# FFN second half as Strassen products over pairs of token tiles, with ff stored by token tile

## The chip, the cores and the metric

The kernel runs on one core of one Trainium2 chip. The metric is the device time of one execution in microseconds. An execution of the kernel before takes 2890.57 us (median of 3 runs, 2889.32 to 2894.1). Names used below: TensorE multiplies matrices into PSUM banks, VectorE and ScalarE work element by element, GpSimd here adds weight blocks and issues some transfers, SyncE (SP) issues most transfers.

## The reference, cut to what matters

An encoder layer (gated recurrence beside dilated attention, both gated by a condition), then a SwiGLU FFN, then a final norm. Two requests of 1024 and 512 tokens are worked on as one matrix of 1536 tokens. Only the FFN and the last norm bear on the change:

```python
D_MODEL = 1024; D_FF = 2816          # 22 column tiles of 128
h2 = _rmsnorm(x, norm2_g) * (1 + sc2) + sh2
fg, fu = jnp.split(h2 @ w_ffn_in, 2, axis=-1)
ff = (silu(fg) * fu) @ w_ffn_out     # (1536, 2816) @ (2816, 1024)
x = x + gt2 * ff
y = _rmsnorm(x, final_g)             # x * rsqrt(mean(x*x) + EPS) * final_g
```

All arrays are float32.

## The kernel before, in words

Every float32 product is made of three TensorE matmuls: each operand is split into a high part (a ScalarE copy to the type fp32r) and a low part (a VectorE subtraction of the high part), and hi x hi, hi x lo and lo x hi are accumulated. `split` (L146 to L149) does this.

The order of all work is written out by hand: instructions stand on each engine in the order of the code, and the engine works them off in that order.

**FFN first half** (L1382 on). 44 steps `p`: 22 column tiles in a first pass over tokens 0 to 767, and again in a second pass over tokens 768 to 1535 (`p % NFF` is the column tile, `p // NFF` the pass). Each step has 7 products `c` of 12 matmuls, Strassen's scheme over halves of the contraction and of the tokens, 384 columns each. The bank of a product is `(P1, P2, P3, P4, P1, P2, P3)[c]`; the fifth to seventh products accumulate onto a bank whose earlier content VectorE or ScalarE has already read. The evacuations are the `if c == ...` chain (L1392 to L1412). At c == 6 the two results, X (tokens of the first half of the pass) and Y (second half), are done and are stored by SP to `ffd`, which is laid out [column tile, 128, token]. `build` makes the weight operands of the products nine products ahead: GpSimd adds two blocks, ScalarE copies, VectorE subtracts. `wraw` loads the weights of a later step into tiles of the tags raw, hi and lo.

**FFN second half** (L1448 on). Three chunks of 512 tokens. For each chunk 11 steps `kp` over pairs of contraction tiles; in each step the transposed ff of 512 tokens (class `Stream`, 512 KB) and two rows of tiles of `w_fo` (class `Slots`, 1 MB) are loaded by SP, split, and multiplied: 4 token tiles by 2 halves of 512 output columns by 2 contraction tiles by 3 matmuls. All 8 PSUM banks are accumulators for the whole chunk, and w_fo is loaded and split again for each chunk. After a chunk `scale` multiplies the banks with the gate gt2 into SBUF, and `post` (run one per step of the next chunk) adds the residual x1, squares with accumulation, makes the reciprocal root (`rstd`, small VectorE operations around one ScalarE root), scales by final_g and stores through GpSimd. The last chunk's last two steps go token tile by token tile, with `post_half` and `post_last` behind them.

Of the kernel before, what the change touches and what calls it, by code (L numbers as in the profile page):

```python
# [10 lines left out]
F32 = mybir.dt.float32  # L11
# [6 lines left out]
P = 128  # L18
# [33 lines left out]
def encoder_kernel(  # L52
# [18 lines left out]
    ffd = dram("ffd", [NFF, P, T])  # L71
# [1157 lines left out]
    ffs = Stream([ffd[2 * n:2 * n + 2, :, cc * CH:(cc + 1) * CH].rearrange("k p n -> p k n")  # L1229
                  for cc in range(NCH) for n in range(NFF // 2)], shape=(P, 2, CH))  # L1230

    class Slots:

        def __init__(self):
            self.nl = self.ns = 0
            self.n = NCH * NFF // 2
            self.raw = None

        def at(self, i):
            a = slot[(3, 2, 1)[i % 3]].rearrange("p (a k n) -> p a k n", a=2, k=2)  # L1240
            return a[:, 0], a[:, 1]

        def load(self, n):
            if self.nl == 0:
                self.first = [wts.tile([P, D], F32, tag="lo", name="foraw") for _ in range(2)]
                for k in range(2):
                    sp.dma_start(out=self.first[k], in_=w_fo[k])
                self.nl = 1
            if self.raw is None and n > 1:
                self.raw = act1.tile([P, 2, 2, D], F32, tag="a", name="foraw")  # L1250
            while self.nl < min(n, self.n):
                kp = 2 * (self.nl % (NFF // 2))
                sp.dma_start(out=self.raw[:, self.nl % 2], in_=w_fo[kp:kp + 2].rearrange("k p n -> p k n"))
                self.nl += 1

        def split(self, n):
            while self.ns < min(n, self.n):
                hi, lo = self.at(self.ns)
                for k in range(2):
                    split(self.raw[:, self.ns % 2, k] if self.ns else self.first[k], hi[:, k], lo[:, k])  # L1260
                self.ns += 1

        def get(self, i):
            self.load(i + 1)
            self.split(i + 1)
            return self.at(i)

        def ahead(self, i):
            self.load(i + 2)
            self.split(i + 2)  # L1270
            self.load(i + 3)
# [363 lines left out]
```

## Time and profile before

| | |
|---|---|
| median of 3 runs | 2890.57 us |
| profiled execution, its own time | 2890.56 us |
| its span | 2888.8 us |
| TensorE busy | 2831.2 us, 98% |
| VectorE busy | 1794.3 us, 62% |
| ScalarE busy | 1182.5 us, 41% |
| GpSimd busy | 551.4 us, 19% |
| TensorE's mean granted clock | 0.991 of full |
| moved by DMA | 316.88 MB, 110 GB/s over the span |

The span runs from the first to the last instruction that the profiler recorded. Busy time is the time in which an engine had at least one instruction under way; a matmul's end is modelled, so that the pace of matmuls is better read from how many there are in a stretch than from the length of one. "Idle before" is the engine's idle time ahead of an instruction, with the engine or transfer whose signal ended it. A transfer's time to landing runs from its issue to the signal that its data has arrived.

### The profile page before, as it was taken

How to read it: one execution, taken by the hardware profiler on the slowest of the kernel's cores; microseconds unless marked ns; L12 is line 12 of the kernel's file. 1: busy time of each engine (PE TensorE's matmuls, PEld its weight loads, DVE VectorE, ACT ScalarE, POOL GpSimd, SP SyncE). 2: the span in 40 equal slices, each digit the busy share in tenths (PEclk: the TensorE clock that was granted, in tenths of full speed). 3: DMA queues.
4: the chain of work that ended last, by engine and by line, in shares of the span. 5: the costliest groups of instructions: out<-in, count | busy, mean ns of one | idle time of the engine just before them, and what ended most of it. 6: DMA issues, size and time to landing. Idle time of an engine off the chain costs nothing. (4 is left out here: it accounts for less than half of the span.)

```text
span 2888.8 us, 37337 instructions
## 1 busy us (share of the span) xinstructions
PE 2831.2 (98%) x14330; PEld 2375.9 (82%) x14330; DVE 1794.3 (62%) x3097; ACT 1182.5 (41%) x2260; POOL 551.4 (19%) x545
## 2 busy tenths in 40 slices
PE   8999999999999999999999999999999999999998
PEld 4878777877777777777778777899999999988886
DVE  6487776555555555553467846677788788635364
ACT  6375666333333333234431015544444334323232
POOL 0000000000000000000243331266544444300001
PEclk9999999999999999999999999999999999999999
DMA  6211011201111111111467754546434333355552
GB/s 235 68 35 66 33 55 45 78 30 34 34 35 37 41 34 35 34 35 54 130 228 259 245 181 130 178 158 188 141 104 166 101 101 101 133 208 167 189 173 90
DMA packets 125155, 316.88 MB, mean 110 GB/s; under 512 B 17096, under 2 KB 48328, under 8 KB 124720
## 3 DMA queue, kind: packets, MB, share of 16 engines
q1 hardware_dynamic: 106736, 252.30, 26.9%
q0 software_dynamic: 17664, 61.14, 6.1%
q8 instruction: 113, 1.85, 0.3%
q10 hardware_dynamic: 576, 1.05, 0.1%
q14 instruction: 66, 0.54, 0.1%
HBM read 242.57 MB, written 71.88 MB: 109 GB/s over the span
## 5 line engine op out<-in xcount | busy, mean ns | idle before, releaser
L158 PE MATMUL mm<-hh,whi 128*128 128x512 f32 x1632 | 663.6, 407 | 1.8 <-DVE hh L291 1.3
L160 PE MATMUL mm<-hh,wlo 128*128 128x512 f32 x1632 | 641.9, 393 | 0.0
L159 PE MATMUL mm<-hl,whi 128*128 128x512 f32 x1632 | 640.7, 393 | 0.5 <-DVE hl L292 0.4
L149 DVE TENSOR_TENSOR wlo<-wraw,whi 128x1024 fp32r<-128x1024 f32 x127 | 155.6, 1230 | 363.9 <-ACT whi L148 363.6
L158 PEld LDWEIGHTS mm<-hh,whi 128*128 128x128 f32 x1632 | 311.8, 191 | 70.4 <-issue 7.2
L160 PEld LDWEIGHTS mm<-hh,wlo 128*128 128x128 f32 x1632 | 308.2, 189 | 68.6
L159 PEld LDWEIGHTS mm<-hl,whi 128*128 128x128 f32 x1632 | 309.4, 190 | 62.6 <-DVE hl L292 3.3
L1296 POOL TENSOR_TENSOR sum<-wf 128x512 f32<-128x512 f32 x220 | 297.7, 1359 | 304.6 <-DVE woh L1307 192.8
L148 ACT CAST whi<-wraw 128x1024 fp32r<-128x1024 f32 (+1 forms) x129 | 131.1, 1017 | 406.5 <-PE sd L1474 175.0
L746 ACT ACTIVATE sm<-sm,sg 128x192 f32<-128x192 f32 (+2 forms) x288 | 114.3, 398 | 303.4 <-DVE sg L741 302.8
L1307 DVE TENSOR_TENSOR woh<-sum,woh 128x512 fp32r<-128x512 f32 x148 | 146.6, 1001 | 48.5 <-ACT woh L1306 48.1
L741 DVE CUSTOM_DVE_ANT_0 sm<-sd,mk 128x192 f32<-128x192 f32 (+2 forms) x288 | 72.9, 291 | 117.0 <-PE sd L734 64.3
L667 DVE SCALAR_TENSOR_TENSOR t<-mm,rp 128x512 f32<-128x512 f32 x72 | 49.8, 692 | 150.3 <-PE mm L160 150.3
L798 POOL DMA_DIRECT2D od<-of x24 | 13.1, 547 | 635.3 <-ACT qb L719 354.4
L1306 ACT CAST woh<-sum 128x512 fp32r<-128x512 f32 x148 | 91.5, 621 | 103.7 <-POOL sum L1296 103.7
L1378 PE MATMUL mm<-top,woh 128*128 128x384 f32 x348 | 116.5, 335 | 3.2 <-ACT top L1367 3.2
L1380 PE MATMUL mm<-top,woh 128*128 128x384 f32 x348 | 116.3, 334 | 0.0
L1379 PE MATMUL mm<-top,woh 128*128 128x384 f32 x348 | 116.2, 334 | 0.0
L856 DVE CUSTOM_DVE_ANT_0 jk<-ada 128x1024 bf16<-128x1024 f32 x64 | 80.5, 1270 | 24.4 <-DMA ada<-in_w_ada_dram 17.2
L1474 PE MATMUL mm<-wol,whi 128*128 128x512 f32 x352 | 94.5, 390 | 0.1
L1474 PE MATMUL sd<-wol,whi 128*128 128x512 f32 x352 | 94.4, 389 | 0.0
L1405 ACT ACTIVATE flat<-flat 128x384 f32<-128x384 f32 x44 | 23.1, 526 | 169.4 <-DVE flat L1404 169.4
(341 smaller groups left out, 6230.2 us busy)
## 6 DMA issues: line engine op xcount, KB each, us to landing
wf<-in_w_fi_dram SPq DMA_DIRECT2D x88, 512.0 KB, 4.5
wraw<-in_w_in_dram SPq DMA_DIRECT2D x68, 512.0 KB, 3.5
foraw<-in_w_fo_dram SPq DMA_DIRECT2D x32, 1024.0 KB, 5.2
ffd<-flat SPq DMA_DIRECT2D x88, 192.0 KB, 4.3
wraw<-ffd SPq DMA_DIRECT2D x33, 512.0 KB, 3.6
ada<-in_w_ada_dram SPq DMA_DIRECT2D x32, 512.0 KB, 3.8
gated<-gs POOLq DMA_DIRECT2D x48, 256.0 KB, 2.7
gt<-gated POOLq DMA_DIRECT2D x48, 256.0 KB, 4.0
```

Of the source, the lines that this page charges most:

```text
L148: s.copy(out=hi, in_=t)
L149: eng.tensor_tensor(out=lo, in0=t, in1=hi.bitcast(F32), op=ALU.subtract)
L158: pe.matmul(ps, lhsT=hi(k), rhs=xh(k), start=a, stop=False)
L159: pe.matmul(ps, lhsT=hi(k), rhs=xl(k), start=False, stop=False)
L160: pe.matmul(ps, lhsT=lo(k), rhs=xh(k), start=False, stop=z)
L746: s.activation(out=sm[:, c], in_=sm[:, c], func=AF.Exp, scale=-1.0, bias=sg[:, u, x:x + 1], accum_out=sg[:, u, x + 1:x + 2])
L1296: g_.tensor_tensor(out=sums[m], in0=wraws[p, a], in1=wraws[p, b], op=op)
L1307: v.tensor_tensor(out=r[:, CH:], in0=t, in1=f32(r[:, :CH]), op=ALU.subtract)
L1378: pe.matmul(ps, lhsT=hi, rhs=bh[:, k], start=k == 0 and not more, stop=False, skip_group_check=more)
L1379: pe.matmul(ps, lhsT=hi, rhs=bl[:, k], start=False, stop=False, skip_group_check=more)
L1380: pe.matmul(ps, lhsT=lo, rhs=bh[:, k], start=False, stop=k == 3, skip_group_check=more)
L1474: pe.matmul(pp[t][e], lhsT=lt[:, k2, cols], rhs=w[:, k2, e * CH:(e + 1) * CH], start=(k == 0 and lt is fh and w is wh), stop=(k == NFF - 1 ...
```

## The change

The first half's arithmetic stays. Its steps take the column tiles in another order (`column`: 0, 11, 1, 12, ...), ff is stored by token tile, [token tile, 128, 22 x 128], and beside it `ffx` holds for each pair of token tiles (t, t + 3) two differences and a sum of blocks of ff. With A11, A12 the two column halves of ff of token tile t, A21, A22 those of token tile t + 3: d0 = A21 - A11, d1 = A12 - A22, s = A21 + A22. VectorE makes them at c == 6 (one operation at even steps, two at odd) and SP stores them.

The second half becomes 7 combinations by 6 pairs of token tiles, 42 steps; a step is one product of 11 contraction tiles by 3 matmuls of 512 columns into one PSUM bank, with its left operand `acmb` (two buffers) and its B pieces (`bslot`, 20 slots). `aload` loads raw left operands two steps ahead, `aprep` splits them one step ahead (in two combinations it adds two operands first, in three pieces); `bload` and `bbuild` load and make B pieces (for five of the seven combinations the sum or difference of two blocks of w_fo) one combination ahead, in a pair of raw buffers. `take` adds the product of the step before into accumulators in SBUF (one tile of 128 x 1024 for each of the 12 token tiles), and as soon as a half of a token tile is complete, `half` applies gate and residual and squares, and `fin` normalises a token tile and stores it. The last product is done in two halves of 256 columns with a short chain behind them.

Cut to its core; of the removed code only the heads are left:

```diff
-    ffd = dram("ffd", [NFF, P, T])
+    ffd = dram("ffd", [NT, P, NFF * P])
+    ffx = dram("ffx", [NT // 2, 3, P, NFF // 2 * P])
...
-    ffs = Stream([ffd[2 * n:2 * n + 2, :, cc * CH:(cc + 1) * CH].rearrange("k p n -> p k n")
-    class Slots:
-    fos = Slots()
...
+    PRODO = (
+        (3, ("11",), ("12", "22", ALU.subtract)),
+        (1, ("11", "22"), ("11", "22", ALU.add)),
+        (5, ("11", "12"), ("22", None, None)),
+        (2, ("s",), ("11", None, None)),
+        (4, ("22",), ("21", "11", ALU.subtract)),
+        (6, ("d0",), ("11", "12", ALU.add)),
+        (7, ("d1",), ("21", "22", ALU.add)),
+    )
+    PAIRS = (0, 1, 2, 6, 7, 8)
+    bslot = [slot[i][:, D * e:D * (e + 1)] for i in (5, 2, 0, 1) for e in range(4)]
+    araw = [f32(slot[i][:, :2 * AH]) for i in (4, 3)]
...
+    def bload(upto):
+        while nbl[0] < min(upto, len(PRODO) * KH):
+            q, k = divmod(nbl[0], KH)
+            t = braw[nbl[0]] = wts.tile([P, D], F32, tag="raw", name="wo2")
+            nbl[0] += 1
+            for e, nm in enumerate(PRODO[q][2][:2]):
+                if nm:
+                    i, j = int(nm[0]) - 1, int(nm[1]) - 1
+                    sp.dma_start(out=t[:, e * CH:(e + 1) * CH], in_=w_fo[KH * i + k, :, j * CH:(j + 1) * CH])
+    def bbuild(upto):
+        while nbb[0] < min(upto, len(PRODO) * KH):
+            n = nbb[0]
+            bload(n + 1)
...
+            t, r = braw.pop(n), bslot[n % 20]
+            op = PRODO[n // KH][2][2]
+            if op is not None:
+                v.tensor_tensor(out=t[:, :CH], in0=t[:, :CH], in1=t[:, CH:], op=op)
+            split(t[:, :CH], r[:, :CH], r[:, CH:])
+            bload(n + 3)
...
+    def aprep(n):
...
+        a, (hi, lo) = araw[n % 2], acmb[n % 2]
+        cut = [slice(o, min(o + CH, AH)) for o in range(0, AH, CH)]
+        if len(PRODO[n // len(PAIRS)][1]) == 1:
+            cut = [slice(0, 6 * P), slice(6 * P, AH)]
+        for c in cut:
+            t = a[:, c]
+            if len(cut) == 3:
+                t = tmp.tile([P, CH], F32, tag="t2", name="asum")[:, :c.stop - c.start]
+                v.tensor_tensor(out=t, in0=a[:, c], in1=a[:, AH + c.start:AH + c.stop], op=ALU.add)
+            split(t, hi[:, c], lo[:, c])
...
+        def ffstore(dst, src):
+            sp.dma_start(out=dst.rearrange("t p n -> p t n"), in_=src.rearrange("p (t n) -> p t n", n=P))
...
-                sp.dma_start(out=ffd[i, :, t0:t0 + HT], in_=X)
+                ffstore(ffd[t0:t0 + 3, :, i * P:(i + 1) * P], X)
...
+            if c == 6:
+                xd = ffx[t0 // 2:t0 // 2 + 3, :, :, i % (NFF // 2) * P:(i % (NFF // 2) + 1) * P]
+                a, b = (X, Y) if p % 2 else (Y, X)
+                v.tensor_tensor(out=u2, in0=a, in1=b, op=ALU.subtract)
+                ffstore(xd[:, p % 2], u2)
+                if p % 2:
+                    v.tensor_tensor(out=r, in0=TX[2], in1=Y, op=ALU.add)
+                    ffstore(xd[:, 2], r)
...
+            if p == 2 * NFF - 3 and c == 6:
+                bload(2)
+            if p == 2 * NFF - 2 and c % 2 == 0:
+                bbuild(c // 2 + 1)
             if p == 2 * NFF - 1:
                 if c == 0:
-                    fos.load(1)
+                    aload(0)
+                if c < 4:
+                    bbuild(5 + c)
                 if c == 1:
+                    aprep(0)
+                if c == 2:
+                    aload(1)
...
+        def half(t, f, xo, ps):
+            a = acc[t][:, f]
+            v.tensor_tensor(out=a, in0=a, in1=gt2[t // 8][:, f], op=ALU.mult)
+            v.tensor_tensor(out=a, in0=a, in1=xo, op=ALU.add)
+            e = f.start // CH
+            s.activation(out=ps, in_=a, func=AF.Square, accum_out=st[:, 2 * t + e:2 * t + e + 1])
...
+        def take(n, ps):
+            q, i = divmod(n, len(PAIRS))
+            c, t1 = PRODO[q][0], PAIRS[i]
+            t2 = t1 + 3
+            if c == 3:
+                s.copy(out=acc[t1][:, F2], in_=ps)
+                s.copy(out=acc[t2][:, F2], in_=ps)
+            elif c == 1:
+                s.copy(out=acc[t1][:, F1], in_=ps)
+                add(t2, F2, ps)
...
+            elif c == 4:
+                add(t2, F1, ps)
+                add(t1, F1, ps)
...
+            return {5: (t1, F2), 4: (t2, F1), 6: (t2, F2), 7: (t1, F1)}.get(c)
...
+        for n in range(NSTEP - 1):
+            q, i = divmod(n, len(PAIRS))
+            before, ps = ps, (sdb if n % 2 else mmb)()
+            done = xo = None
+            for k in range(KH):
+                mms(ps, n, k)
+                if k == 0:
+                    if n == 0:
+                        bbuild(KH)
+                    aprep(n + 1)
+                    aload(n + 2)
+                elif k == 2:
+                    if n:
+                        done = take(n - 1, before)
+                    if done:
+                        xo = x1load(*done)
+                elif k in (4, 7):
+                    t = (q + 1) * KH + (2, 4, 6, 8, 9, 11)[i] if n > 2 else KH + 3 * n
+                    bbuild(t - 1 if k == 4 else t)
...
+                elif k == 9:
+                    if done:
+                        half(*done, xo, before)
+                        if (done[0] in PAIRS) == (done[1] is F1):
+                            fins.append(done[0])
+                    for _ in range({5: i % 2, 6: 2}.get(q, 0)):
+                        if fins:
+                            fin(fins.popleft())
...
+        n = NSTEP - 1
+        for e, pl in enumerate((sdb(), mmb())):
+            cols = slice(256 * e, 256 * e + 256)
...
+            for k in range(KH):
+                mms(pl, n, k, cols)
...
```

## Rows read from the trace of the kernel before

**Rows 1.** Stretches, core 0: us; busy us (instructions) by engine; PEclk, DMA share, GB/s.
```profile
2245.00:2489.00 244.00, 244.00 (x1410) 244.00 (x1409) 197.02 (x257) 97.77 (x189) 112.74 (x85) 1.00 0.32 97
2488.40:2503.00 14.60, 14.60 (x86) 14.60 (x85) 10.21 (x16) 5.83 (x12) 3.89 (x3) 1.00 0.08 28
2517.50:2877.50 360.00, 359.88 (x1584) 297.08 (x1584) 167.03 (x226) 114.38 (x153) 20.23 (x31) 1.00 0.51 173
2877.50:2888.80 11.30, 0.02 (x1) 0.00 (x0) 5.98 (x14) 3.32 (x9) 2.09 (x2) 0.71 0.25 93
```

**Rows 2.** Chain of waits, one piece of the second half: start us, us, work.
```profile
2523.64 5.44 PE sd L1474 x24
```

**Rows 3.** Groups of instructions, VectorE, from 2517.5 us on.
```profile
L1500 DVE TENSOR_TENSOR xo<-xo,xs 128x512 f32<-128x512 f32 x16 | 10.3, 684 | 0.0
...
L1491 DVE TENSOR_TENSOR xs<-mm,gt 128x512 f32<-128x512 f32 x8 | 5.0, 680 | 0.0
```

**Rows 4.** Groups of instructions, ScalarE, whole span.
```profile
L148 ACT CAST wol<-foraw 128x1024 fp32r<-128x1024 f32 x44 | 44.1, 1048 | 3.8 <-DMA foraw<-in_w_fo_dram 3.8
...
L1306 ACT CAST woh<-sum 128x512 fp32r<-128x512 f32 x148 | 91.5, 621 | 103.7 <-POOL sum L1296 103.7
...
L1367 ACT CAST top<-top 128x768 fp32r<-128x768 f32 x10 | 7.8, 831 | 0.2 <-DMA top<-h2d 0.2
```

**Rows 5.** Timeline of VectorE in column tile 42: start, length, operation [idle before].
```profile
2496.36 0.68 DVE L1307 TENSOR_TENSOR wol<-sum,wol 128x512 fp32r<-128x512 f32 x1
...
2496.96 0.55 DVE L1400 TENSOR_TENSOR flat<-sd,flat 128x384 f32<-128x384 f32 x1
...
2497.43 0.68 DVE L1307 TENSOR_TENSOR wol<-sum,wol 128x512 fp32r<-128x512 f32 x1
...
2502.55 0.69 DVE L1307 TENSOR_TENSOR wol<-wf,wol 128x512 fp32r<-128x512 f32 x1 [1.10 <-ACT wol L1306]
```

**Rows 6.** Timeline of VectorE and ScalarE in one token tile's normalisation.
```profile
2663.80 1.29 DVE L1500 TENSOR_TENSOR xo<-xo,xs 128x512 f32<-128x512 f32 x2
...
2664.52 0.63 ACT L1501 ACTIVATE xs<-xo 128x512 f32<-128x512 f32 x1 [2.27 <-DVE xo L1500]
...
2665.89 0.16 DVE L1503 TENSOR_TENSOR st<-st 128x1 f32<-128x1 f32 x1 [0.80 <-ACT xs L1501]
...
2666.51 0.16 DVE L168 RECIPROCAL st<-st 128x1 f32<-128x1 f32 x1 [0.27 <-ACT st L167]
...
2667.48 1.42 DVE L1507 SCALAR_TENSOR_TENSOR xo<-xo,st,fgb 128x512 f32<-128x512 f32 x2
```

**Rows 7.** DMA issues: transfer, queue, count, KB each, median us to landing.
```profile
foraw<-in_w_fo_dram SPq DMA_DIRECT2D x32, 1024.0 KB, 5.2
...
ffd<-flat SPq DMA_DIRECT2D x88, 192.0 KB, 4.3
...
wraw<-ffd SPq DMA_DIRECT2D x33, 512.0 KB, 3.6
...
gated<-gs POOLq DMA_DIRECT2D x48, 256.0 KB, 2.7
...
ring<-od SPq DMA_DIRECT2D x36, 256.0 KB, 3.5
...
wraw<-in_w_brb_dram SPq DMA_DIRECT2D x8, 256.0 KB, 6.2
```

**Rows 8.** Stretches around two gaps of TensorE, columns as in Rows 1.
```profile
1784.00:1790.00 6.00, 3.86 (x20) 2.96 (x19) 5.89 (x11) 3.40 (x6) 1.64 (x1) 1.00 0.51 170
1790.00:1796.00 6.00, 6.00 (x24) 4.79 (x23) 4.00 (x7) 3.58 (x9) 2.90 (x2) 0.72 0.01 3
2195.00:2201.00 6.00, 2.83 (x17) 2.51 (x16) 4.63 (x6) 5.26 (x10) 3.97 (x3) 1.00 0.00 0
2201.00:2207.00 6.00, 5.97 (x34) 5.91 (x35) 5.93 (x9) 2.22 (x5) 3.23 (x2) 1.00 0.36 131
```

**Rows 9.** Timeline, the last store's issue.
```profile
2885.18 0.34 ACTq L1531 DMA_DIRECT2D out_dram<-xs  x1
```

More of the change, by code (lines that the diff above doesn't have):

```diff
@@ new lines, in aload @@
+    def aload(n):
+        if n >= NSTEP:
+            return
+        q, i = divmod(n, len(PAIRS))
+        if n == 0:
+            a0["raw"] = upper
+            for nm in ("hi", "lo"):
+                a0[nm] = [wts.tile([P, D], F32R, tag=nm, name="a0" + nm) for _ in range(2)]
+            bslot.extend(a0["hi"] + a0["lo"])
+            for e, (o, w) in enumerate(((0, D), (D, AH - D))):
+                sp.dma_start(out=a0["raw"][e][:, :w], in_=asrc("11", 0)[:, o:o + w])
+            return
+        for e, nm in enumerate(PRODO[q][1]):
+            sp.dma_start(out=araw[n % 2][:, e * AH:(e + 1) * AH], in_=asrc(nm, i))
@@ new lines, in aprep @@
+    def aprep(n):
+        if n >= NSTEP:
+            return
+        if n == 0:
+            for e, w in enumerate((D, AH - D)):
+                split(*(a0[nm][e][:, :w] for nm in ("raw", "hi", "lo")))
+            return
+        a, (hi, lo) = araw[n % 2], acmb[n % 2]
[8 more added lines that the diff above has]
+            split(t, hi[:, c], lo[:, c])
@@ L1274, in encoder_kernel, with apart, column @@
+    def apart(n, k):
+        if n:
+            return tuple(a[:, k * P:(k + 1) * P] for a in acmb[n % 2])
+        e, o = divmod(k, 8)
+        return tuple(a0[nm][e][:, o * P:(o + 1) * P] for nm in ("hi", "lo"))
+    def column(p):
+        return p % NFF // 2 + NFF // 2 * (p % 2)
     wraws = {}
@@ new lines, in encoder_kernel, with dest, add, x1load @@
+        gt2 = [po.tile([P, D], F32, name=f"gt{q}") for q in range(2)]
+        F1, F2 = slice(0, CH), slice(CH, D)
+        def dest(t):
+            return y_prompt[0, t * P:(t + 1) * P, :] if t < 8 else y_sample[0, (t - 8) * P:(t - 7) * P, :]
+        def add(t, f, ps, op=ALU.add):
+            a = acc[t][:, f]
+            v.tensor_tensor(out=a, in0=a, in1=ps, op=op)
+        nx = [0]
+        def x1load(t, f):
+            e, m = divmod(nx[0] % 4, 2)
+            nx[0] += 1
+            a = upper[e][:, m * CH:(m + 1) * CH]
+            sp.dma_start(out=a, in_=x1d[t * P:(t + 1) * P, f])
+            return a
@@ new lines, in operands, with mms @@
+        def operands(n, k):
+            b = bslot[(n // len(PAIRS) * KH + k) % 20]
+            return apart(n, k) + (b[:, :CH], b[:, CH:])
+        def mms(ps, n, k, cols=slice(0, CH)):
+            hi, lo, bh, bl = operands(n, k)
+            pe.matmul(ps, lhsT=hi, rhs=bh[:, cols], start=k == 0, stop=False)
+            pe.matmul(ps, lhsT=hi, rhs=bl[:, cols], start=False, stop=False)
+            pe.matmul(ps, lhsT=lo, rhs=bh[:, cols], start=False, stop=k == KH - 1)
+        fins = deque()
+        ps = None
@@ new lines, in encoder_kernel @@
+        n = NSTEP - 1
+        b = wts.tile([P, CH], F32, tag="raw", name="b")
+        for e, pl in enumerate((sdb(), mmb())):
+            cols = slice(256 * e, 256 * e + 256)
+            pl = pl[:, cols]
+            for k in range(KH):
+                mms(pl, n, k, cols)
+                if e == 0 and k == 4:
+                    done = take(n - 1, ps)
+                    half(*done, x1load(*done), ps)
+                    fins.append(done[0])
+                if e == 0 and k == 9:
+                    while fins:
+                        fin(fins.popleft())
+            v.tensor_tensor(out=b[:, cols], in0=pl, in1=gt2[1][:, cols], op=ALU.mult)
+            v.tensor_tensor(out=a[:, cols], in0=a[:, cols], in1=b[:, cols], op=ALU.add)
+            s.activation(out=pl, in_=a[:, cols], func=AF.Square, accum_out=st[:, 60 + e:61 + e])
+            v.tensor_tensor(out=b[:, cols], in0=a[:, cols], in1=fgb[:, cols], op=ALU.mult)
+            if e == 0:
+                v.tensor_tensor(out=st[:, 62:63], in0=st[:, 60:61], in1=st[:, 2 * tl + 1:2 * tl + 2], op=ALU.add)
```

193 lines of the change are left out of this document (60 added, 133 removed).

## The prediction

> **What bounds the kernel now.** I first read the busy table by engine, which has TensorE at 98% of the span, then the stretches, the chain of waits, and the groups of VectorE and ScalarE. The second half of the FFN, the part that the change rewrites, runs from 2517.5 to 2877.5 us. TensorE is busy in 359.9 of its 360 us, with 1584 matmuls, so one per 227 ns; VectorE is busy 167 us of it [rows 1]. The chain is a row of 24-matmul pieces of 5.44 us with nothing between them [rows 2]. TensorE sets this stage and the other engines have room. The FFN's first half is the same: 1410 matmuls in 244 us, 173 ns each, VectorE busy 197 [rows 1]. After the last matmul 11.3 us of normalising and storing remain [rows 1, 9].
>
> **What goes from TensorE.** Seven products of 11 contraction tiles replace eight. 42 products (7 combinations by 6 pairs) of 33 matmuls are 1386 at 227 ns, 314.9 us. One product is 7.49 us. The last one runs as 66 matmuls of 256 columns; no row has that width, so by the line through 384 columns (173 ns) and 512 (227 ns) I take 120 ns, 7.9 us together (113, half of 227, to 173 ns as bounds: 7.5 to 11.4). TensorE saves 359.9 - 314.9 - 0.4 = 44.6 us. Everything else is about how much is given back.
>
> **What VectorE gets.** An operation of 512 columns takes 0.68 from SBUF or PSUM [rows 3], and the next independent one starts 0.60 after it (0.47 for 384 columns) [rows 5]. ScalarE's copy takes 0.62 for 512 columns and 0.83 for 768 [rows 4]; hand-overs cost 0.03 to 0.04 (sum ends 2664.49, Square starts 2664.52) [rows 6]. Both engines work in program order, so a VectorE operation that waits for ScalarE holds all behind it.
> - A B piece with a sum is sum, copy, subtract, one after the other: 0.72 + 0.66 + 0.60 = 1.98. Without a sum the copy runs ahead: 0.60. Five of the seven combinations have a sum: 55 pieces of 77.
> - Splitting a left operand (768 and 640 columns) is 0.86 + 0.73 = 1.6, on the line through 0.47 and 0.60 [rows 5]. Its first copy queues on ScalarE behind the Square of the step before: VectorE waits 0.66 + 0.83 = 1.6 where a residual half was last, 0.2 to 0.3 elsewhere, nothing behind a normalisation. With two operands (combinations 1 and 5) three pieces of sum, copy, subtract: 2 x 1.98 + 1.58 = 5.5.
> - Each accumulator addition 0.62. A residual half, two dependent operations, 0.72 + 0.65 = 1.37. A normalisation: from 2665.89 to the end of the row pair at 2667.48 + 1.42, 3.0 [rows 6], plus 0.4 behind a Square, 0.8 behind its own.
>
> In step n VectorE prepares operand n+1, takes product n-1, builds one to three B pieces for the next combination, then does a residual half and normalisations. Summed per combination (six steps, 44.9 us of TensorE): 43.6 in the second, 51.6 in the third, 41.2 in the fourth, 52.0 in the fifth, 60.7 in the sixth (three normalisations); the seventh's five whole steps are 43.7 against 37.4 (seven normalisations). An example, a step of combination 4: 1.6 wait + 1.6 split + 1.25 two additions + 2 x 1.98 + 1.37 = 9.8 against 7.49.
>
> **What of it delays TensorE.** The next operand is ready 2 to 2.5 us into VectorE's step, so VectorE may be 5 us behind before TensorE waits. I carry this forward: VectorE's step n starts when its step n-1 and product n-1 have ended, and product n starts when product n-1 and the first piece of operand n have. The second to fifth combinations cost 5 us, as the slack takes most of it; the sixth 14; the seventh 8.
>
> **The start.** Pieces 0 to 7 are built inside the first half's last two column tiles. There are two raw buffers: SP loads piece n+2 when VectorE has read piece n. For a pair of 256 KB loads I take 3.8 (3.5 of the nearest row, loads of the same size on SP, and a later second issue; bounds 2.7 and 6.2 [rows 7]). In us from 2517.5: the first load stands on SP behind the two new stores and lands at -21.5, and VectorE waits at piece 0. The tile's other work had left it only some 4.4 us (14.6 - 10.2 [rows 1]) against the 8 of four pieces; they end at -19.5, -15.2, -11.0, -5.7. Piece 4 ends at -3.7; piece 5 waits for its load until -1.8 and ends at 0.2; operand 0 is split by 2.3. Only then comes the addition at L1397 that reads the bank of the seventh product: due at -2.1, that starts at 2.8 and ends at 4.9. Pieces 6 and 7 and the rest of the first half last until 12.1, pieces 8, 9, 10 end at 14.1, 16.1, 19.9. So the first product ends at 20.6 instead of 7.5. Steps 1 and 2 have three pieces each, again at the refill's pace; product 5 ends at 61.0 instead of 44.9. The start costs 16 us. [...]
>
> **The first half's additions.** Each column tile gets a subtraction, each second one an addition: 0.47 to 0.55 each, 0.8 per 14.6 us. They stand where VectorE now waits (1.10 for ScalarE [rows 5]; 47 of 244 us idle [rows 1]), and the builds are nine products ahead: I take nothing. The addition reads the buffer of the tile before, so ScalarE's copy into it (L1393) may wait for it, and behind that copy the builds' copies, all with those nine products (19 us) in hand. If the cover were gone it would be 44 x 0.8 = 35 us. The 154 stores of 192 KB in 512-byte rows (88 now, 4.3 us to land [rows 7]) have 14 us until their buffers are needed. At the change of pass, where VectorE is fullest, a stall could grow by 0 to 2. Operand loads of 704 KB lie between 3.6 and 5.2 us [rows 7] with over 7 us to land, residual loads earlier still: nothing, 0 to 3 where a step loads two operands.
>
> **The end.** The last step's VectorE work (take, half, normalisation, 5.7 us) starts at 358.3, and the last tile's chain and its store end 8.2 after it: 372.2, which is 13.8 after the last matmul at 358.4. Now it is 11.3: 2.5 more.
>
> **Sum.** -44.6 + 16 + 5 + 14 + 8 + 2.5 = +0.9; unrounded 1.3. The profiled execution took 2890.56 (span 2888.8), 0.01 from the median of 2890.57. Forecast 2892, no change that can be measured: 0.2% (5.8 us) is about what a measurement of this kernel can tell.
>
> **Rivals.**
> - Waits covered: ScalarE runs further ahead than I allow, refills land in 2.7, and TensorE stays the bound but in the sixth and seventh combinations. For it: ScalarE is busy only 114 of the stage's 360 us [rows 1]. Against it: sum, copy and subtract are one chain, whoever is idle. Losses 5 + 0 + 8 + 3, end +0: -44.6 + 16 = -29, 2862.
> - Late refills (slower): the piece loads share the queues with 704 KB operand loads and the first half's stores, and land in 6.2 as the slowest 256 KB row did [rows 7]. It decides from about 4.5 us on, where the third piece of a step waits longer than two are built. 2.4 more for each of some eight refills on the start's path: 2892 + 19 = 2911.
> - Clock: TensorE now gets gaps of 2 us and more, about nine by my ledger. After one gap of 2.14 us the next 6 us had a granted clock of 0.72 (between the levels of 1.2 and 2.4 GHz) and 24 matmuls, where the rate of the stretch before (20 in 3.86 us) gives 31; after one of 3.17 us it stayed at 1.00 [rows 8]. Seven matmuls at 193 ns are 1.35 us, nine gaps at most 12: 2904. Where VectorE sets the pace a slower product is hidden, which speaks against it. The Trainium skill ("TensorE: Matmul & The Clock Gate", Part 1) says that the array is throttled by default and activity releases it; the 0.72 agrees, the 3.17 us gap shows that not each gap pays.
>
> **How the numbers follow.** Forecast 0.42 (own range 2882 to 2902: 0.09 faster, 0.26 same, 0.07 slower), waits covered 0.27 (2850 to 2878, faster), late refills 0.16 (slower), clock 0.15 (0.05 same, 0.10 slower). Faster 0.36, same 0.31, slower 0.33. From 2858 to 2908 about 0.1 is left out at either end.
>
> **What would show it.** VectorE's busy time in the last stage rises from 167 to about 280 us and it idles there for ScalarE; TensorE has some 40 us of idle, most of it before products 0 to 4 and in the last two combinations, released by VectorE; the seventh product of column tile 43 waits for L1397's addition. Wrong, if TensorE idles less than 20 us in the stage, or waits mostly for a DMA or on ScalarE, or if the first half grows by more than 5 us.

## The result, and the profile after

The kernel after takes 2964.46 us (median of 4 runs, 2960.05 to 2966.2), the kernel before beside it 2892.34. The ratio is 1.0247, 95% interval [1.0234, 1.0259]: slower by 72 us, where no change was forecast, and outside the forecast's own range of 2882 to 2902. The profiled execution's span is 2962.6 us.

TensorE's busy time fell from 2831.2 to 2827.5 us only, VectorE's rose from 1794.3 to 1974.3. The stretches of the kernel after that answer to the second half, the end and the steady first half in [rows 1], columns as there:

```profile
2245.00:2489.00 244.00, 231.47 (x1324) 228.92 (x1323) 212.73 (x261) 88.58 (x175) 104.70 (x79) 1.00 0.39 113
2573.65:2947.35 373.70, 342.65 (x1420) 267.38 (x1419) 253.92 (x437) 132.97 (x245) 10.86 (x20) 0.96 0.65 220
2947.35:2962.60 15.25, 0.00 (x0) 0.00 (x0) 9.13 (x28) 2.87 (x9) 1.08 (x2) 0.61 0.23 86
```

First line: in the first half, which the change hardly touches, TensorE gets through 1324 matmuls in 244 us instead of 1410. A pair of column tiles (168 matmuls) takes 31.0 us, 29.1 before. Second line: the second half starts 56 us late, at 2573.65 instead of 2517.5, and lasts 373.7 us to its last matmul, 13.7 more than all of the old one. Third line: 15.25 us behind the last matmul.

Against the predicted timeline, in us: the first product was to end 20.6 after 2517.5 and ended 70.3 after it (+49.7); from there to the last matmul 337.8 were due and 359.5 measured (+21.7); behind it 13.8 and 15.25 (+1.4). Together 72.8, all of the miss. To split the 49.7 I follow one mark through all kernels: the last Silu of column tile 41, the last tile before the pieces of the second half are built. It starts at 2488.41 in the kernel before and at 2533.62 in the one after, 45.2 late.

**Where a pair of tiles loses its time.** Timeline of the kernel after at the start of an even tile (start us, us, work, idle before):

```profile
2319.43 1.53 POOL L1352 TENSOR_TENSOR sum<-wf 128x512 f32<-128x512 f32 x1 [5.01 <-DVE woh L1363]
...
2319.73 1.63 DVE L1484 TENSOR_TENSOR flat<-flat 128x384 f32<-128x384 f32 x1
...
2321.45 0.48 ACT L1452 COPY flat<-mm 128x384 f32<-128x384 f32 x1 [4.05 <-issue]
...
2321.98 0.44 PE L1434 MATMUL mm<-top,woh 128*128 128x384 f32 x1 [1.60 <-ACT flat L1452]
...
2322.48 0.69 DVE L1363 TENSOR_TENSOR woh<-sum,woh 128x512 fp32r<-128x512 f32 x1 [1.11 <-ACT woh L1362]
```

VectorE's sum over the pair (L1484) reads Y of the even tile. ScalarE's copy into that same buffer for the next even tile (L1452) may not start before the sum has ended; it starts 0.09 after it, 4.05 us idle. ("issue" says that the profile names no releaser: that it is the sum is read from the code and tested by e2.) TensorE's fifth product accumulates onto the bank that this copy reads, and waits 1.60. VectorE in turn finds no copy ready (1.11). In 2240 to 2500 us this is TensorE's only listed wait:

```profile
PE mm L1434 <- ACT flat L1452: 12.5, 8, 1.6
```

**The second half.** Waits of the kernel after from 2573.6 to 2948 us (engine, what waits <- for what: us in total, times, longest); PE is TensorE; the last five lines are SP's queue from 2573 on:

```profile
ACT woh L149 <- DVE wo L1274: 41.9, 21, 3.9
DVE a0lo L150 <- ACT a0hi L149: 35.3, 29, 6.1
ACT sd L1546 <- DVE acc L1544: 33.5, 11, 4.8
ACT mm L1546 <- DVE acc L1544: 32.8, 11, 4.8
...
PE sd L1588 <- ACT a1hi L149: 9.5, 10, 1.8
...
PE sd L1590 <- DVE a1lo L150: 7.8, 6, 1.8
PE mm L1588 <- ACT a0hi L149: 7.2, 7, 1.9
...
SPq L1263 <- DVE woh L150: 91.8, 29, 8.3
SPq L1263 <- DVE slot L150: 45.1, 11, 11.6
SPq L1263 <- DVE wol L150: 44.3, 15, 6.9
...
SPq L1263 <- DVE a0lo L150: 17.7, 6, 6.9
SPq L1263 <- DVE a0hi L150: 17.3, 6, 7.0
```

ScalarE's Squares (L1546) stand waiting for VectorE with the next operand's copies behind them, as predicted. New is SP: its piece loads (L1263) wait some 216 us for VectorE to free a raw buffer, and every operand load stands in the same queue behind them. TensorE idles 31 us of the stage, 20 of them for ScalarE's copies and 10 for VectorE's subtractions. So two of the prediction's signs of being wrong are there: TensorE waits mostly on ScalarE, and the first half grew by far more than 5 us.

### The profile page after: what moved, and what is told of

Its sections match the earlier page's. It is cut to its first block, busy times and chain, and to the rows that moved or that the text cites. A ratio compares the mean times of both kernels' runs of the same rounds, so it can differ in the third digit from the quotient of the medians.

```text
span 2962.6 us, 38009 instructions
## 1 busy us (share of the span) xinstructions
PE 2827.5 (95%) x14165; PEld 2352.2 (79%) x14165; DVE 1974.3 (67%) x3399; ACT 1197.2 (40%) x2359; POOL 540.6 (18%) x532
## 5 line engine op out<-in xcount | busy, mean ns | idle before, releaser
L160 PEld LDWEIGHTS mm<-hl,whi 128*128 128x128 f32 x1632 | 309.6, 190 | 62.7 <-DVE hl L293 3.3
L150 DVE TENSOR_TENSOR wlo<-wraw,whi 128x1024 fp32r<-128x1024 f32 x94 | 115.3, 1234 | 191.7 <-ACT whi L149 191.7
L1363 DVE TENSOR_TENSOR woh<-sum,woh 128x512 fp32r<-128x512 f32 x148 | 165.9, 1123 | 30.1 <-ACT woh L1362 28.4
L149 ACT CAST whi<-wraw 128x1024 fp32r<-128x1024 f32 x96 | 96.3, 1005 | 198.9 <-PE mm L160 119.5
L668 DVE SCALAR_TENSOR_TENSOR t<-mm,rp 128x512 f32<-128x512 f32 x72 | 49.8, 692 | 150.3 <-PE mm L161 150.3
L1434 PEld LDWEIGHTS mm<-top,woh 128*128 128x128 f32 x348 | 66.4, 191 | 32.4 <-ACT flat L1452 21.7
L1363 DVE TENSOR_TENSOR wol<-sum,wol 128x512 fp32r<-128x512 f32 x72 | 80.3, 1116 | 10.6 <-ACT wol L1362 9.5
```

The costliest lines, as they stand in the source:

```text
L149: s.copy(out=hi, in_=t)
L150: eng.tensor_tensor(out=lo, in0=t, in1=hi.bitcast(F32), op=ALU.subtract)
L160: pe.matmul(ps, lhsT=hi(k), rhs=xl(k), start=False, stop=False)
L1363: v.tensor_tensor(out=r[:, CH:], in0=t, in1=f32(r[:, :CH]), op=ALU.subtract)
L1434: pe.matmul(ps, lhsT=hi, rhs=bh[:, k], start=k == 0 and not more, stop=False, skip_group_check=more)
```

## The experiments

Three theories for the first half: *buffer* (the copy that waits for the sum, above), *full loop* (weight sums go from GpSimd over ScalarE to VectorE through two buffers, with so little to spare that each added VectorE operation costs its length), *stores* (66 more stores). For the second half: *VectorE* (steps as long as its work) or *queue* (operand loads behind piece loads). All times are of one run each beside the kernel before (2890.9 to 2894.4), unless an interval is given. "Tile 41" is how late the mark is against the kernel before; steps are measured from the first matmul of each product in the timeline. Two spreads help to judge single runs: the first tile's Silu, which stands before all that is changed here, lies 3.0 us early to 3.5 late against the kernel before, and six kernels with the same second half (after, e1 to e5) need 370.0 to 374.1 for it.

| kernel | us | tile 41 | first product at | to last matmul | the seven combinations |
|---|---|---|---|---|---|
| after | 2964.5 | 45.2 | 2573.6 | 373.7 | 59.0 52.4 53.5 47.2 50.5 57.8 53.3 |
| e1 | 2915.3 | 2.8 | 2528.1 | 370.0 | 57.2 49.2 55.1 46.8 49.1 60.9 51.7 |
| e2 | 2939.0 | 18.4 | 2547.9 | 374.1 | 60.0 51.5 53.7 47.2 48.7 59.7 53.3 |
| e3 | 2913.6 | -1.1 | 2526.0 | 370.5 | 56.5 51.1 54.7 47.2 48.5 60.8 51.7 |
| e4 | 2951.7 | 37.7 | 2565.7 | 370.5 | 56.1 50.9 53.4 47.2 49.0 60.8 53.2 |
| e5 | 3003.8 | 84.8 | 2613.4 | 373.3 | 57.8 50.0 55.7 47.3 49.5 62.5 50.6 |
| e6 | 2996.3 | | 2618.1 | 361.2 | 62.1 46.5 54.9 44.9 46.6 53.9 52.3 |
| e7 | 3003.3 | | 2623.1 | 361.7 | 55.7 47.7 52.1 47.2 46.4 60.9 51.7 |
| e8 | 3036.6 | | 2622.4 | 397.3 | 66.9 52.4 60.1 47.8 55.7 63.6 50.6 |
| g1 | 2950.8 | 13.8 | 2539.6 | 394.2 | 55.9 64.6 65.1 47.2 50.5 59.0 51.9 |
| g2 | 2943.0 | 8.1 | 2538.8 | 387.2 | 58.1 59.5 63.9 45.9 52.4 53.9 53.4 |
| g3 | 2933.2 | 9.6 | 2540.8 | 375.4 | 57.2 60.4 62.7 45.2 44.9 52.0 53.0 |
| g4 | 2924.7 | 12.3 | 2532.3 | 374.2 | 51.8 44.9 59.4 61.6 50.0 51.8 54.6 |
| h1 | 2904.1 | 17.7 | 2538.1 | 349.0 | 50.2 46.4 45.0 57.0 47.9 52.0 50.6 |
| h2 | 2883.1 | 12.1 | 2532.4 | 333.7 | 50.8 44.9 45.2 55.7 44.9 44.9 47.3 |
| h3 | 2877.8 | 9.3 | 2526.6 | 331.3 | 51.1 44.9 44.9 52.7 44.9 44.9 48.0 |
| k1 | 2954.0 | 48.1 | 2576.2 | 360.7 | 51.7 50.0 54.6 47.2 44.9 60.6 51.7 |
| k2 | 2896.1 | 10.8 | 2527.6 | 351.5 | 49.8 44.9 44.9 61.1 49.0 51.9 49.8 |

TensorE's own time is 44.9 for a combination and 45.3 for the last.

### e1 and e3: without the additions; without them but with their stores

```diff
-                v.tensor_tensor(out=u2, in0=a, in1=b, op=ALU.subtract)
                 ffstore(xd[:, p % 2], u2)                    # e1: removed too
                 if p % 2:
-                    v.tensor_tensor(out=r, in0=TX[2], in1=Y, op=ALU.add)
                     ffstore(xd[:, 2], r)                     # e1: removed too
```

> Leaves out the two differences and the sum per pair of column tiles and their stores; the second half reads ff itself in their place, so the same bytes are loaded. In the kernel after, a pair of column tiles takes 31.0 us in the second pass where it took 29.1 before, and the first half 704.7 us where it took 648.5; the time is 2964.5. All three theories say that the additions or their stores are the cause, so here all expect a pair of 29.1 to 29.3 us, a first half of 657 to 662 (11 of the 56 us stand at its very end, where B pieces are built), and a time of 2915 to 2922. If the pair stays near 31, the cause is what the change keeps here: the order of the column tiles or the stores of ff in rows of 512 bytes.

> The difference and sum operations are left out, their 66 stores of 192 KB stay (what they store is not the difference or the sum). Store theory: pair 30.8 to 31.0 us, time about 2962. Buffer and full-loop theories: pair 29.1 to 29.4, time 2915 to 2925.

The stretch 2320 to 2500 us, in the kernel after:

```profile
2320.00:2500.00 180.00, 170.31 (x975) 168.39 (x974) 158.39 (x191) 65.27 (x128) 79.02 (x60) 1.00 0.39 112
```

in e1:

```profile
2320.00:2500.00 180.00, 180.00 (x1040) 180.00 (x1039) 144.33 (x184) 71.63 (x136) 79.28 (x62) 1.00 0.34 94
```

in e3:

```profile
2320.00:2500.00 180.00, 180.00 (x1040) 180.00 (x1039) 144.50 (x186) 70.62 (x134) 79.69 (x62) 1.00 0.40 116
```

1040 matmuls are 29.1 us a pair, 975 are 31.0. The stores cost nothing: that theory falls, and with it the order of the column tiles, which e1 and e3 keep. The operations, at 14 us of VectorE's 180, cost 42 to 46 us of the kernel's time (tile 41: 45.2 late against 2.8 and -1.1).

### e2 and e4: more buffers for Y; more for the weight sums

```diff
-            X, Y, u2, r = TX[p % 2], TX[2 + p % 2], ...
+            X, Y, u2, r = TX[p % 2], YB[p % 4], ...              # e2
...
-                sums[m] = tmp.tile([P, CH], F32, tag="t2", name="sum")   # two buffers
+                sums[m] = (two of tmp, two in free parts of flat)[...]   # e4
```

> All the work of the kernel after; only Y, the tile's second result, has four buffers instead of two, so that ScalarE's copy into it no longer waits for the sum over a pair. Buffer theory (ScalarE's copy waits for the sum, and TensorE's fifth product waits for that copy, 1.60 us a pair): pair 29.1 to 29.4 us, time 2916 to 2924. Full-loop theory (VectorE had only 0.4 us to spare per column tile, since it waits for the two buffers of weight sums, so each added operation costs its length; 1.7 us a pair less 0.8): pair 30.2 to 30.6, time 2945 to 2955. Store theory: 31.0, 2962.

> All the work of the kernel after; from column tile 4 on the weight sums that GpSimd makes for ScalarE and VectorE have four buffers instead of two; Y keeps its two. Full-loop theory: the loop of GpSimd, ScalarE and VectorE is loosened, VectorE is no longer behind, pair 29.1 to 29.5 us, time 2917 to 2925. Buffer theory: the copy still waits for the sum behind the builds on VectorE, pair 30.5 to 31.0, time 2950 to 2964. Store theory: 31.0, 2962.

In e2 a new buffer lies over a part of the last token tile's rows that is still to be read in column tile 2, so that those 128 tokens are computed from other values; the later kernels use it from tile 4 on. The stretch in e2:

```profile
2320.00:2500.00 180.00, 179.96 (x1034) 178.74 (x1034) 163.35 (x202) 68.44 (x134) 86.57 (x63) 1.00 0.40 114
```

and in e4:

```profile
2320.00:2500.00 180.00, 173.84 (x995) 171.92 (x993) 159.39 (x197) 61.60 (x126) 82.97 (x59) 1.00 0.39 113
```

A pair takes 29.2 in e2 and 30.4 in e4. So the buffer is the cause of the wait at each pair: with VectorE doing the same work (163 of 180 us), TensorE runs through. But only 27 of the 45 us come back. The marks show where the rest is: tiles 4 to 13 and 24 to 33 of the kernel before follow each other at 14.14 to 14.17 us, those of e2 at 14.67 to 14.73. There each tile loses some 0.55 us, 10 us in all, as the loop theory asks. Where the kernel before itself needs 14.56 (tiles 14 to 18 and 33 to 41), e2 loses only 0.15 a tile. Another 2.8 us are e2's lateness at the first tile already.

### e5: the additions on GpSimd

```diff
-                v.tensor_tensor(out=u2, in0=a, in1=b, op=ALU.subtract)
+                g_.tensor_tensor(out=u2, in0=a, in1=b, op=ALU.subtract)
```

and the same for the sum, on top of the four Y buffers.

> All the work of the kernel after; Y in four buffers from column tile 4 on, and GpSimd instead of VectorE makes the two differences and the sum of a pair. With four Y buffers alone the second half's first product began at 2547.9 us, without the operations at 2528.1. If the 20 us left are VectorE's time for the operations (full-loop theory, in the stretches where VectorE is fullest: first pass, change of pass, last two column tiles), it begins at 2526 to 2531 and the time is 2914 to 2919. If they are the operations wherever they run (a read of X and Y that holds a buffer), it begins at 2540 to 2548, and the time is 2930 to 2939.

Both theories missed: it is 39 us slower than the kernel after. GpSimd's waits in 2320 to 2500 us of e5:

```profile
POOL flat L1482 <- issue: 66.4, 12, 5.5
```

GpSimd works in program order. Its subtraction waits 5.5 us in each tile, by the code until VectorE has made Y (the profile names no releaser), and the weight sums of all later builds are queued behind it. An engine that is 18% busy over the span of the kernel after was still the wrong place.

### e6, e7, e8: GpSimd makes the second half's sums; it issues the piece loads; both

```diff
-                v.tensor_tensor(out=t[:, :CH], in0=t[:, :CH], in1=t[:, CH:], op=op)
+                g_.tensor_tensor(out=t[:, :CH], in0=t[:, :CH], in1=t[:, CH:], op=op)      # e6, e8; asum too
...
-                    sp.dma_start(out=t[:, e * CH:(e + 1) * CH], in_=w_fo[...])
+                    g_.dma_start(out=t[:, e * CH:(e + 1) * CH], in_=w_fo[...])            # e7, e8
```

All three on top of e5, so only the second half counts.

> As the one with four Y buffers and GpSimd's differences; in the second half GpSimd also makes the sums of the B pieces and of the two-operand left operands (55 pieces of 512 columns and 36 operand pieces), some 58 us less for VectorE at 0.62 to 0.68 each. From the start of the second half's first product to its last matmul it takes 370 to 374 us in all kernels so far. VectorE theory (steps are long because VectorE works late): 350 to 360 us, time 2895 to 2905. Queue theory (steps are long because the operand loads stand on SP behind piece loads that wait for VectorE to free a raw buffer): 364 to 371, time 2908 to 2916. Latency theory (GpSimd's sum takes twice as long, and the chain sum, copy, subtract sets the pace): over 374, time over 2919.

> As the one with four Y buffers and GpSimd's differences; the loads of B pieces stand on GpSimd's queue instead of SP's, so that an operand load no longer waits behind them. From the start of the second half's first product to its last matmul: queue theory 350 to 360 us, time 2895 to 2905; VectorE theory 366 to 373, time 2910 to 2918.

> Both edits of the second half together: GpSimd makes the sums and issues the piece loads. VectorE theory: as with GpSimd's sums alone, within 4 us. Queue theory: as with the moved loads alone, within 4. If both hold: 335 to 348 us from the first product to the last matmul, time 2880 to 2893. If GpSimd, which now holds sum and load in one order, sets the pace: over 360, time over 2905.

Each edit alone takes 12 us off the 373.3 (361.2 and 361.7), just short of what its own theory asked and more than the other allowed. So both causes are there. e6 gains in combinations 2, 4, 5 and 6, whose steps have sums or follow them, and loses 4 in the first; e7 gains in the first three and the fifth. Together they lose 24, since loads that wait for VectorE now hold the sums in GpSimd's order (e8 from 2620 to 2990 us):

```profile
ACT woh L149 <- POOL wo L1274: 63.3, 16, 8.4
POOL wo L1263 <- DVE woh L150: 61.3, 27, 3.9
```

### g1 to g4: operand loads on ScalarE's queue, then one more edit each

All have VectorE's additions again, three Y buffers, and three, from tile 16 on five, buffers of weight sums.

```diff
-            sp.dma_start(out=araw[n % 2][:, e * AH:(e + 1) * AH], in_=asrc(nm, i))
+            s.dma_start(out=araw[n % 2][:, e * AH:(e + 1) * AH], in_=asrc(nm, i))         # g1
+   second half's sums on GpSimd, as e6                                                    # g2
+   the Square of a residual half is issued in the next step, behind the operand's copies  # g3
...
     PRODO = (
+        (2, ("s",), ("11", None, None)),                                                  # g4
         (3, ("11",), ("12", "22", ALU.subtract)),
```

> All the work of the kernel after, differences and sum on VectorE again. Y has three buffers and the weight sums three, later five (from column tile 4 and 16 on); in the second half the operand loads stand on ScalarE's queue, so that they never stand behind a piece load on SP. First half: with four Y buffers alone the second half's first product began at 2547.9 us, with the differences on GpSimd at 2613. If the rest is the loop through the two sum buffers, it begins at 2532 to 2541 now; if VectorE itself is full, at 2544 to 2549. Second half, from the first product to the last matmul: queue theory 358 to 364 us as with the piece loads on GpSimd's queue (361.7); if GpSimd's queue helped for another reason, 370 to 374.

> As the one with operand loads on ScalarE's queue, and GpSimd makes the sums of the B pieces and operands of the second half. With sums on GpSimd and all loads on SP the second half took 361.2 us; with sums and piece loads both on GpSimd 397. If queue and VectorE are two separate causes, they add up now that no transfer waits behind a sum: 344 to 353 us from the first product to the last matmul. If they are one cause, 358 to 363.

> As the one before in this list, and the Square of a residual half stands on ScalarE behind the next step's operand copies instead of before them. In the kernel after ScalarE waits 39 and 35 us for VectorE's residual addition with the next operand's copies queued behind it. If that wait holds TensorE: combinations 4 to 7 (by order of work) come down to 45 to 48 us each, 6 to 14 us off the second half. If VectorE is behind anyway: within 3 us of the kernel without this edit.

> As the one before in this list, with the combination whose B pieces need no sum (product 2, operand s) put first, so that the eight pieces built inside the first half's last two column tiles cost VectorE 0.6 us each and not a chain of sum, copy and subtraction; the accumulators' first writes change with it. Start theory (those chains delay the end of the first half and the first product): the second half's first product begins 5 to 10 us earlier and the first combination takes 46 to 52 us instead of 56 to 62; the time comes out at 2868 to 2892, faster than before or equal. If the start is set by the piece loads through two raw buffers: within 4 us of the kernel without this edit.

First half: in g1 to g3, which share it, tile 41 is 8 to 14 late and the first product begins at 2539 to 2541, as the loop theory said. Second half: g1 and g2 missed by 30 us and more. The two combinations with two operands, 46 to 56 us in all kernels before with all loads on SP, take 60 to 65. g3 came as expected in its sum: the last four combinations take 195.1 instead of 205.6, so ScalarE's Squares did hold the operands; but most of it is the fifth (52.4 to 44.9), and the sixth and seventh stay at 52 and 53, not 45 to 48. In g4 the first product begins 8.5 us earlier and the first combination takes 51.8 instead of 57.2, as the start theory said. Its pieces lack the sum and also the second of their two loads, so g4 does not tell the chain of sum, copy and subtraction from the loads. It missed its time: at a ratio of 1.0118 [1.0101, 1.0135] it is still slower than the kernel before. Why a step with two operands takes 10 us, 2.4 more than the same step in h1 below, is seen in g4's waits from 2629 to 2750 us:

```profile
ACT a1hi L149 <- POOL asum L1317: 37.4, 18, 6.1
ACT a0hi L149 <- POOL asum L1317: 31.1, 15, 5.4
POOL asum L1317 <- DMA wol<-ffd: 26.4, 5, 7.3
POOL asum L1317 <- DMA slot<-ffd: 24.7, 5, 6.2
```

ScalarE issues the next load behind copies that wait for sums that wait for the load before.

### h1, h2, h3: loads first; the piece's sum in its own buffer; GpSimd's additions later

```diff
-                    aprep(n + 1)
                     aload(n + 2)
+                    aprep(n + 1)                                                          # h1
...
-                g_.tensor_tensor(out=t[:, :CH], in0=t[:, :CH], in1=t[:, CH:], op=op)
+                a, t = t, tmp.tile([P, CH], F32, tag="t2", name="bsum")                   # h2
+                g_.tensor_tensor(out=t, in0=a[:, :CH], in1=a[:, CH:], op=op)
...
+            if c == 2:                                                                    # h3
+                (difference and sum of the tile before, on g_)
```

> As the last kernel of the list before (product 2 first, 2924.7 us), with one change: in each step ScalarE issues the operand loads for two steps ahead before the copies of the next operand, not behind them. There the two combinations with two operands took 59.4 and 61.6 us. If the loads' place in the queue is the cause, they come down to 46 to 52 us each and the time to 2898 to 2912. If 1.4 MB a step is more than the transfers can bring in 7.5 us, they stay at 57 or more, time 2918 to 2926.

> As the kernel with the loads issued first, with the sum of a B piece written to a buffer of its own, so that the raw buffer is free for the next load after GpSimd's sum and not after VectorE's subtraction. In the kernel with product 2 first GpSimd waits 62 us for piece loads in the last three combinations, which take 50.0, 51.8 and 50.5 us. If the two raw buffers set that pace: 2 to 4 us less in each of these, time 5 to 10 us less than with the loads issued first. If VectorE sets it: within 3 us.

> As the kernel with the sums in a buffer of their own, and the differences and sums of the first half made by GpSimd in the next column tile, behind its third product, where X and Y have been ready for some 5 us (with four Y buffers from tile 16 on). With GpSimd making them at once the first half was 50 us longer. If it was GpSimd's wait for X and Y, with the weight sums queued behind it, the second half's first product begins at 2520 to 2527 now, against 2532, and the time is 2885 to 2900. If GpSimd's own time is the matter (1 us an operation), it begins at 2540 or later, and the time is over 2905.

h1: the first combination with two operands falls from 59.4 to 45.0, with the same bytes, so it was the place in the queue; the second, which also builds pieces with sums, only to 57.0. h2 brought 21 us where 5 to 10 were expected, 15.3 of them in the second half; the other 5.7 lie before its first product, in code that h1 has too. The fifth and sixth combination run at TensorE's pace, the last within 2 us of it. The fifth and sixth, in the kernel after:

```profile
2785.15:2835.67 50.52, 47.67 (x200) 38.04 (x199) 34.53 (x51) 18.44 (x32) 0.00 (x0) 0.97 0.66 217
2835.67:2893.50 57.83, 49.37 (x200) 37.55 (x199) 40.92 (x72) 20.81 (x38) 2.21 (x4) 0.97 0.61 210
```

in h2:

```profile
2729.00:2773.90 44.90, 44.90 (x200) 37.17 (x199) 44.01 (x50) 20.20 (x38) 18.64 (x13) 1.00 0.81 285
2773.90:2818.80 44.90, 44.90 (x200) 37.18 (x199) 44.18 (x54) 19.86 (x36) 17.95 (x13) 1.00 0.78 264
```

VectorE is now busy 44 of the 44.9 us, more than in the kernel after (34.5 of 50.5 and 40.9 of 57.8). There it idled 16 to 17 us of each, in a ring of raw buffer, load, sum, copy and subtraction. Busy time misleads here, though: in the fifth combination VectorE has 51 operations in the kernel after and 50 in h2, but beside GpSimd's sums they are longer (the product with the gate 685 ns against 1603; see the last section).

h3 gives GpSimd the same operations as e5, three products later. It runs at 2877.82 us, ratio 0.9949 [0.9932, 0.9965]: 0.5% faster than the kernel before, 86.6 us under the kernel after. Its own step over h2, 5 us, is no more than single runs of one kernel differ by. Against e5 it has up to five buffers of weight sums instead of two as well, and its GpSimd still stands idle 53 of 180 us before these operations (66 in e5); how much is due to the later place and how much to the buffers no run separates. The steady stretch and the second half in h3:

```profile
2320.00:2500.00 180.00, 180.00 (x1041) 180.00 (x1040) 155.40 (x192) 68.37 (x137) 122.80 (x81) 1.00 0.39 111
2526.60:2858.00 331.40, 319.05 (x1421) 260.87 (x1419) 256.33 (x349) 132.94 (x244) 142.58 (x113) 1.00 0.72 253
```

### k1 and k2: the own buffer alone; the sums back on VectorE

k1 is the kernel after with h2's edit, the sum on VectorE; k2 is h3 with the second half's sums on VectorE.

> The kernel after with one edit: VectorE writes the sum of a B piece to a buffer of its own, so that the raw buffer is free after that sum and not after the subtraction that follows ScalarE's copy. In the kernel after the second half takes 373.7 us from its first product to the last matmul. If the held raw buffers (through the loads that queue on SP behind them) are a cause by themselves: 355 to 366 us, time 2942 to 2956. If VectorE's own work sets the pace of these steps, each piece frees its buffer only some 1.3 us earlier on a VectorE that is late anyway: 370 to 374, time 2959 to 2964.

> The fastest kernel (2877.8 us) with the sums of B pieces and operands in the second half back on VectorE. The second half took 331.3 us from the first product to the last matmul, with combinations 5 and 6 at 44.9 us, TensorE's own time. If VectorE's work is a bound of its own beside the buffers and queues: the combinations whose steps build pieces with sums or have two operands (3 to 6 by order of work) take 48 to 56 us each, and the second half 345 to 365, time 2892 to 2912. If buffers and queues were all: within 5 us of the fastest kernel.

The held raw buffer cost 13 us by itself (360.7 against 373.7; the first combination 59.0 to 51.7, the fifth 50.5 to 44.9). k2 needs 20 us more than h3, all of it in the fourth to seventh combination. So with the buffers and queues mended, sums on VectorE still cost. But it is not that VectorE is full. Its busy time in k2's second half,

```profile
2527.60:2879.10 351.50, 328.31 (x1421) 265.33 (x1419) 256.65 (x441) 134.02 (x244) 13.54 (x22) 0.98 0.69 238
```

is that of h3 above (256.33), and in the fourth to sixth combination it is busy 125.0 of 162.1 us, in h3 130.3 of 142.5. What k2 has more of is the chain: sum, ScalarE's copy and subtraction one after the other on an engine that works in order, with its waits, as the prediction's ledger had it.

## Why the prediction was wrong, step by step

- **"The first half's additions ... I take nothing"**: this step failed, and carries 45 of the 72.8 us (tile 41; 42 against e1). The case "if the cover were gone" was priced there at 35 and given no chance. Three readings were wrong in it. The sentence on the buffer named the copy that waits, and then put "nine products in hand" against it: but the copy also frees the bank of TensorE's fifth product, four products later, and no lead in weights covers that. VectorE's 47 idle us of 244 were read as room; they were its share of the waiting in a ring with GpSimd and ScalarE, with two buffers, and e2 shows how little was left (0.55 us lost per tile wherever the kernel before needs 14.15 for one). And the price was taken from the tile of [rows 5], where GpSimd is busy 3.89 of 14.6 us [rows 1]: the sum took 1.63 on average, not 0.55 (below); the difference took 0.55 to 0.58, about as priced. Both together are 59 us of VectorE in the first half, not 35.
- **The start**: right in kind, 4.5 us short (70.3 - 45.2 = 25.1 against 20.6). The seventh product waits 4.73 us for the predicted addition, and 2569.04 is its start:

```profile
2569.04 0.55 DVE L1456 TENSOR_TENSOR flat<-sd,flat 128x384 f32<-128x384 f32 x1
...
2569.64 0.69 PE L1434 MATMUL sd<-slot,wol 128*128 128x384 f32 x1 [4.73 <-DVE flat L1456]
```

  The rest of the first combination took 44.8 for 40.4. g4 bears the cause out as far as it goes: pieces without sums, and with one load instead of two, bring 8.5 + 5.4 us.
- **"The second to fifth combinations cost 5 us"**: they cost 24 (52.4 + 53.5 + 47.2 + 50.5 against 4 x 44.9). VectorE's work was not under-counted (busy 253.9 us of the stage; some 280 predicted), yet the second and fourth, where its 43.6 and 41.2 us were to fit, took 52.4 and 47.2. What the step left out are queues and buffers: "operand loads ... nothing, 0 to 3" counted the time to land (4.9 to 6.3 us) and not the place on SP behind piece loads that wait for VectorE. Over the whole second half, moving the piece loads off SP (e7) gives 12 us back and freeing the raw buffer earlier (k1) 13; k2, which has h3's queues, buffers and order but the sums on VectorE, wins 22 of the 59 us lost against TensorE's own time.
- **The sixth, 14, and the seventh, 8**: 12.9 and 8.0 measured. Right in size, and in part for VectorE's chain as argued: in k2, with the sums on VectorE, 7.0 and 4.5 us of it remain; in h2, with the sums on GpSimd, nothing and 2.0. The rest went with the other edits (queues, buffers, the Squares' place), most of which the step did not have, so that the sizes agree is in part luck. (0.66 + 0.83, the wait behind a Square, is 1.5 and not 1.6; it changes little.)
- **TensorE's saving**: as predicted, 7.48 us a step where nothing waits, 3.9 to 4.1 for the last half product (7.9 for both). Nowhere does it reach the time whole: h3 comes nearest, 331.3 + 15.2 behind it against 371.3 before: 24.8 of the 44.6.
- **The end**, 13.8: 15.25.
- **The rivals**: *waits covered* (2862) is what h3 comes within 16 us of, and that takes nine edits. *Late refills*: a load landed in 3.1 us (median; the second of a pair is issued 0.4 later), so the 3.8 taken for a pair was enough; the loads were not slow but issued late. *Clock*: it came out near its price, beside the other losses and not in their place. The granted clock is 0.96 over the second half and 1.00 in h3. After the wait of 4.73 us above it is 0.50, the lower of its two levels (1.2 GHz), and matmuls of 384 columns start 0.32 us apart instead of 0.17. Counted in the timeline of the second half, 59 matmuls start 0.40 to 0.445 us after the one before with no wait listed, where 0.23 is usual and 0.43 was the pace at 0.50; that is some 12 us (the rival had "at most 12"). In h3 there is one.

## What to carry to other kernels

Idle time of an engine inside a ring of buffers is not room: before an operation is called hidden, name every buffer that it reads and follow who must wait to overwrite it, up to the banks of the engine that sets the pace. An engine that works in order needs operations whose inputs are ready, so work moved to an idle engine can hold up all that stands behind it (e5); h3, where it is issued later and with more buffers ahead, does not lose by it. A load helps only if nothing that waits stands before it in its queue (g4 against h1). Release a load buffer after its first reader, by writing the result elsewhere (h2, k1), before adding engines.

## What the runs showed of the hardware

VectorE's operations with both inputs in SBUF are much longer when they run while GpSimd adds. Groups of VectorE in 2245 to 2489 us of the kernel after (GpSimd busy 104.7 us):

```profile
L1363 DVE TENSOR_TENSOR woh<-sum,woh 128x512 fp32r<-128x512 f32 x53 | 62.3, 1176 | 8.5 <-ACT woh L1362 7.9
...
L1484 DVE TENSOR_TENSOR flat<-flat 128x384 f32<-128x384 f32 x8 | 13.1, 1632 | 0.0
...
L1467 DVE TENSOR_TENSOR flat<-flat,mm 128x384 f32<-128x384 f32 x17 | 9.3, 547 | 0.0
```

and in its second half (GpSimd nearly idle):

```profile
L150 DVE TENSOR_TENSOR woh<-wo,woh 128x512 fp32r<-128x512 f32 x29 | 19.8, 690 | 14.5 <-ACT woh L149 14.5
```

The same subtraction takes 1176 ns beside GpSimd's additions and 690 without them; with one input in PSUM (L1467) it stays at 547. In the timeline above, GpSimd's addition runs from 2319.43 to 2320.96 and the sum, begun at 2319.73, ends 0.40 after that, as if it had stood still until then. The Trainium skill ("SBUF — State Buffer", Who interferes with whom) says that a VectorE instruction with two SBUF inputs contends with a GpSimd instruction that reads SBUF, and that the later one blocks. The trace agrees. The other direction shows too, as far as averages can: in the same stretch GpSimd's weight sums take 1330 ns on average in the kernel before and 1589 to 1639 in h3, where the shortest took 1258; no run isolates the cause.
